# One decoder pass on one core: attention, mLSTM and HGRN products of two heads in turn on the halves of TensorE, GpSimd left out of some stretches, larger first loads

## The chip, the core and the metric

The kernel runs on one core of a Trainium2 chip. It is launched once, reads all inputs from HBM and writes one output of 256 x 1024 numbers. The metric is the device time of an execution in microseconds (us): the median of the runs shown. A profile is one execution taken by the hardware profiler; its time is given beside it.

The engines of the core have short names in the rows: PE is TensorE (matrix products; PEld its weight loads), DVE is VectorE, ACT is ScalarE, POOL is GpSimd, SP issues most DMAs. Each has its own stream of instructions, which it works through in the order of the program; semaphores order them against each other.

## What is computed

Two transformer blocks run one after the other on 256 tokens of width 1024 (T = 256, D = 1024). All is fp32 from outside. The reference, cut to its order of calls:

```python
def first_block(x, mem, ...):
    h = token_mixer(rmsnorm(x, norm_mix_pre), w_in, b_in, ...)       # mLSTM, short conv, MoBA attention, HGRN2; 4 heads of 64 each
    x = x + rmsnorm(h, norm_mix_post)
    h = memory_cross_attention(rmsnorm(x, norm_cross_pre), rmsnorm(mem, mem_norm), wq, wk, wv, wo)   # 4 heads of 128
    x = x + rmsnorm(h, norm_cross_post)
    h = conv_glu_ffn(rmsnorm(x, norm_ffn_pre), w_ffn_in, conv_w, conv_b, w_ffn_out)                  # width 2816
    return x + rmsnorm(h, norm_ffn_post)

def second_block(x, ...):
    h = x + hybrid_mixer(rmsnorm_2(x, norm_mix), w_in, fox_f_bias, ...)   # fox: 8 heads, causal with decay; nsa: 8 heads, two key groups
    h = h + peer_ffn(rmsnorm_2(h, norm_ffn), wq, subkeys, u, v)           # 128 x 128 experts, 8 heads, top 16
    return rmsnorm_2(h, norm_final)
```

In an attention head the scores are q k^T over a head width of 64, a bias is added (MoBA: a relative bias with mask; fox: a decay c_t - c_s and the causal mask; nsa: the causal mask), a softmax over the row follows, and the probabilities multiply the values, again 64 wide. mLSTM forms such a matrix with exponential gates in place of a softmax, and HGRN2 forms one from the decayed products of its gates.

## The kernel before

Activations lie transposed: features on the 128 partitions, eight blocks of them, and the 256 tokens along the free dimension. A dense product of fp32 weights and activations is three products in the format float32r: each operand is split in a high half (a rounded copy) and a low half (the rest), and `mm3` (lines 342 to 347) does high x high (L345), high weight x low activation (L346) and low weight x high activation (L347). `fm_pair` makes two blocks of 128 output features, 48 such products.

Weights stream through `whalf` (L315): a DMA on SP's queue brings 512 KB (tile w), ScalarE copies the high half (wh, recorded at L366 as all of ScalarE's work), and the low half (wl, L324) is w - wh, made by GpSimd for every third half (`wi % 3 == 2`) and by VectorE for the others. Four buffers of each let this run ahead of the products. In the two expert stages at the end `uvnext` (L1040 on) does the same with the expert matrices (uv, uvh, uvl at L1048).

The stages follow each other: start and first norm; `block1_mixer`; `cross`; `ffn`; `block2`; `peer_q`; `peer`. A normalization needs the sum over all features. `norm_sums` (L450) squares four pairs of blocks on ScalarE and adds them on GpSimd (L463); a product with a constant matrix (onesd, L466) sums over partitions, and `rstd` (L432) with three VectorE steps makes the root. At the end of a sub-layer `post_pair` (L489) does this for its output, and `post_norm` (L520) updates x in four pairs (L537, L538; the last pair on GpSimd) and makes the two halves of the next input, xnh on ScalarE and xnl on VectorE (L542). The order of VectorE's work is written out by hand there. `head_norm` does the like for heads.

The order of the instructions on each engine is fixed when the program is built: a planner (`schedule_with_timeline_sim`) simulates the times of all engines and picks what is ready; `issue_after` and `self.behind` force one instruction behind another. Generators (moba, lstm, levels, fox, nsa, memory, cmp) let the source weave steps of attention between dense products.

`attention` (L1626) is used three times: moba (one pair of chunks, 4 heads), fox (two pairs, 8 heads), nsa (two pairs, 8 heads, two branches). A chunk `ch` holds two heads, one in partitions 0 to 63 and one in 64 to 127. A step takes the two heads in the same half `i` of two chunks. Its `scores` (L1642) multiply 64 rows by 128 queries against 128 keys for the first block of queries (S0) and 256 for the second (S1); biases are added by further products into the same PSUM tile (moba L1479; fox decay L811 with 128 rows of LT and RT, most of them zero; causal mask L814); `softmax_rows` (L1620, L1624) and four scalings follow. `values` transposes the probabilities (L1665), copies them (attPT, by ScalarE) and multiplies them with the values into 64 partitions of `po` (L1671, L1672). There are 2 steps for moba, 4 for fox and 8 for nsa. While the scores of a step are worked on by VectorE and ScalarE, the values of the step before and dense products run on TensorE.

HGRN's decay levels (L1423) already take the two heads of a chunk in turn, one in each row half. mLSTM (L1488 on) goes head by head: its gate rows (L1492), its scores (L1500, L1501), then for two heads the numerator and the denominator (L1513, L1514). HGRN's output is three products per head (L1562 to L1564).

At the start (L596 on) x comes in four DMAs of 256 KB and the first weights in two, in turn; each row of such a DMA is 2 KB.

## Time and profile before

| what | value |
|---|---|
| runs, us | 1524.4, 1528.95, 1523.76; median 1524.4 |
| profiled execution, us | 1525.86 |
| its span (first to last instruction), us | 1524.0 |
| TensorE busy | 1477.3 us, 97% |
| VectorE busy | 1078.9 us, 71% |
| ScalarE busy | 777.5 us, 51% |
| GpSimd busy | 323.5 us, 21% |
| mean granted TensorE clock | 0.988 of 2.4 GHz |
| moved by DMA | 246.6 MB, mean 162 GB/s |

Busy shares are means over stages that have different limits, so the table only says where to look. A busy TensorE is one with a product in flight: products are pipelined, and the duration of one (0.28 us for 256 columns in float32r) is longer than the distance between the starts of two. The profile names what ended each wait. On TensorE an fp32 product is recorded as two instructions, a float32r one as one.

### The profile page before, as it was taken

What the parts mean: (1) busy time and instruction counts of PE and PEld (TensorE: products, weight loads), DVE (VectorE), ACT (ScalarE), POOL (GpSimd) and SP (SyncE); (2) the same over time, 40 slices, a digit from 0 to 9 for tenths busy, and PEclk for the clock granted to TensorE, in tenths of its full rate; (3) what the DMA queues carried; (4) which work ended last, traced back from release to release, by engine and by line L of the source; (5) the groups of instructions that cost most, each with busy time, mean ns of one, the idle gap of its engine ahead of it and who ended that gap; (6) DMA issues with size and microseconds to landing.
All of it is one profiled execution on the core that took longest, in us unless ns stands there. A gap on an engine that the chain in (4) does not pass through costs nothing.

```text
span 1524.0 us, 26760 instructions
## 1 busy us (share of the span) xinstructions
PE 1477.3 (97%) x10594; PEld 1364.8 (90%) x10594; DVE 1078.9 (71%) x1930; ACT 777.5 (51%) x1311; POOL 323.5 (21%) x193
## 2 busy tenths in 40 slices
PE   7999989999999999998999999999999999999997
PEld 6888978999998888898999999999999888888886
DVE  6768677766777455557997988878887555555555
ACT  5536556444555555446454545544445555555554
POOL 3733343323224241116352220000000000000001
PEclk9999989999999999999999999999999999999999
DMA  7442432455653353346255455545546555555553
GB/s 239 133 166 92 155 114 77 151 190 178 193 170 125 111 161 100 101 150 230 78 163 186 159 163 177 168 163 167 166 165 205 197 193 193 194 193 193 194 194 124
DMA packets 68679, 246.63 MB, mean 162 GB/s; under 512 B 7589, under 2 KB 8617, under 8 KB 68297
## 3 DMA queue, kind: packets, MB, share of 16 engines
q1 hardware_dynamic: 67976, 243.08, 48.4%
q8 instruction: 83, 1.36, 0.4%
q10 hardware_dynamic: 576, 1.84, 0.3%
q14 instruction: 44, 0.35, 0.1%
HBM read 242.79 MB, written 2.10 MB: 161 GB/s over the span
## 4 chain that ended last, share of the span: by engine, by line
PE 72%; DVE 10%; ACT 2%; DMA 1%; issue 1%; POOL 1%; SPq 0%; DVEq 0%; ACTq 0%; POOLq 0%
PE acc L345 19%; PE acc L346 19%; PE acc L347 19%; PE att L346 3%; PE att L347 3%; PE att L345 3%; PE att L1194 2%; DVE wl L324 1%; DMA uv<-in_U_dram 1%; PE att L1642 1%; DVE xnl L542 1%; PE acc L1671 1%; DVE uvl L1048 1%; DVE tmp L988 1%; POOL uvl L1048 1%
## 5 line engine op out<-in xcount | busy, mean ns | idle before, releaser
L1048 DVE TENSOR_TENSOR uvl<-uv,uvh 128x1024 fp32r<-128x1024 f32 x234 | 289.5, 1238 | 155.1 <-ACT uvh L366 154.9
L366 ACT ACTIVATE uvh<-uv 128x1024 fp32r<-128x1024 f32 x256 | 270.1, 1056 | 232.4 <-PE acc L346 125.2
L366 ACT ACTIVATE wh<-w 128x1024 fp32r<-128x1024 f32 x187 | 195.7, 1056 | 231.1 <-PE acc L346 101.7
L345 PE MATMUL acc<-hh,uvh 128*128 128x256 f32 x1024 | 293.9, 287 | 0.0
L347 PE MATMUL acc<-hh,uvl 128*128 128x256 f32 x1024 | 289.9, 283 | 1.5 <-DVE uvl L1048 1.0
L346 PE MATMUL acc<-hl,uvh 128*128 128x256 f32 x1024 | 289.8, 283 | 0.0
L324 POOL TENSOR_TENSOR wl<-w,wh 128x1024 fp32r<-128x1024 f32 x63 | 158.2, 2511 | 353.0 <-ACT wh L366 320.8
L324 DVE TENSOR_TENSOR wl<-w,wh 128x1024 fp32r<-128x1024 f32 x124 | 165.0, 1337 | 79.2 <-ACT wh L366 76.2
L346 PE MATMUL acc<-uvl,ch 128*128 128x512 f32 x512 | 199.2, 389 | 0.0
L347 PE MATMUL acc<-uvh,cl 128*128 128x512 f32 x512 | 199.2, 389 | 0.0
L347 PEld LDWEIGHTS acc<-hh,uvl 128*128 128x128 f32 x1024 | 195.9, 191 | 2.6 <-POOL uvl L1048 1.3
L346 PEld LDWEIGHTS acc<-hl,uvh 128*128 128x128 f32 x1024 | 196.1, 191 | 0.0
L345 PEld LDWEIGHTS acc<-hh,uvh 128*128 128x128 f32 x1024 | 196.0, 191 | 0.0
L345 PE MATMUL acc<-xnh,wh 128*128 128x256 f32 x544 | 162.4, 299 | 8.4 <-ACT xnh L366 8.4
L346 PE MATMUL acc<-xnl,wh 128*128 128x256 f32 x544 | 161.0, 296 | 6.0 <-DVE xnl L340 3.7
L347 PE MATMUL acc<-xnh,wl 128*128 128x256 f32 x544 | 158.3, 291 | 0.0
L345 PE MATMUL acc<-uvh,ch 128*128 128x512 f32 x512 | 138.5, 389 | 0.0
L1273 POOL TENSOR_TENSOR fin<-fin,gn 128x512 f32<-128x512 f32 x4 | 5.2, 1288 | 588.2 <-ACT sq L366 588.1
L345 PEld LDWEIGHTS acc<-xnh,wh 128*128 128x128 f32 x544 | 107.9, 199 | 11.8 <-ACT xnh L366 8.9
L346 PEld LDWEIGHTS acc<-xnl,wh 128*128 128x128 f32 x544 | 108.0, 198 | 10.4 <-DVE xnl L340 5.4
L346 PE MATMUL att<-xnl,wh 128*128 128x256 f32 x368 | 106.4, 289 | 8.6 <-DVE xnl L542 8.6
L346 PEld LDWEIGHTS acc<-uvl,ch 128*128 128x128 f32 x512 | 96.1, 188 | 20.0
(440 smaller groups left out, 3161.5 us busy)
## 6 DMA issues: line engine op xcount, KB each, us to landing
w<-in_W_dram SPq DMA_DIRECT2D x191, 512.0 KB, 4.0
uv<-in_U_dram SPq DMA_DIRECT2D x128, 512.0 KB, 3.6
uv<-in_V_dram SPq DMA_DIRECT2D x128, 512.0 KB, 3.5
x<-in_xT_dram SPq DMA_DIRECT2D x4, 256.0 KB, 6.3
mem<-in_memT_dram SPq DMA_DIRECT2D x1, 1024.0 KB, 6.5
sk<-in_W_dram SPq DMA_DIRECT2D x1, 1024.0 KB, 7.2
xd<-xt SPq DMA_DIRECT2D x2, 512.0 KB, 5.2
fin<-xd ACTq DMA_DIRECT2D x2, 512.0 KB, 7.2
```

Source lines behind the costliest of these rows:

```text
L324: (self.nc.gpsimd if pool else self.nc.vector).tensor_tensor(out=lo, in0=w, in1=hi.bitcast(F32), op=ALU.subtract)
L345: mm(ps, wsl(w[0]), xsl(x[0]), start=first, stop=False, **k)
L346: mm(ps, wsl(w[0]), xsl(x[1]), start=False, stop=False, **k)
L347: mm(ps, wsl(w[1]), xsl(x[0]), start=False, stop=last, **k)
L366: return self.nc.scalar.activation(out, in_, f, **k)
L542: nc.vector.scalar_tensor_tensor(n.halves[1][:, k], x[:, k], gain[:, k:k + 1], n.halves[0][:, k].bitcast(F32), op0=ALU.mult, op1=ALU.subtract)
L988: nc.vector.match_replace(tmp[:, :n], vals[:, 0:8], src, -3.0e38)
L1048: i = (nc.gpsimd if lo_pool else nc.vector).tensor_tensor(out=lo, in0=w, in1=hi.bitcast(F32), op=ALU.subtract)
L1194: mm(ps[:, j], m1[:, j], m2[:, s * NT + j], start=s == 0, stop=s == 1)
L1273: nc.gpsimd.tensor_tensor(out=half[b][n], in0=half[b][n], in1=gn[:, n * 512:(n + 1) * 512], op=ALU.mult)
L1642: mm(S[:, c], q[r, ch, blk * 128:(blk + 1) * 128], k[r, br if nsa else ch, :128 * (blk + 1)], start=c == 0, stop=False, skip_group_check=True)
L1671: mm(po[r, c], v[:, 0, vc:vc + 64], PT[:, 0:256], start=not nsa, stop=False, skip_group_check=True)
```

## The change

1. `attention`: a step now takes the two heads of one chunk. Scores, fox decay and values of the two heads are issued in turn, on the two row halves (scores, decay) or column halves (values) of the array; each head has its own PSUM tile for scores. The second to fourth products of a group are put behind the first. For the decay, LT and RT hold their rows twice, once in each half. The maxima and sums of the softmax are taken per head and block of queries.
2. mLSTM: the scores of two heads, and then numerator and denominator, alternate in the same way. HGRN's output products alternate between heads.
3. A flag `calm`: while it is set, no low half of a weight is made by GpSimd. It is set at the start, from the end of the mixer to the queries of cross attention, from its output product until the FFN's fourth step, from the FFN's step 19 or output product 8 until fox attention begins, and from the output product of block 2 until the first query pair of PEER; in the other PEER pairs every second half (before: every third) goes to GpSimd.
4. The sums of squares (L463, L500), the product of two gains and the last pair in `post_norm` move from GpSimd to VectorE.
5. Start: x comes in two DMAs of 512 KB and the first weights in one (rows of 4 KB); eight products of constants are issued on TensorE before anything has landed.

```diff
@@ constants
-        er[h, h] = 1.0
-        el[32 + h, h] = -1.0
+        er[h, h] = er[64 + h, h] = 1.0
+        el[32 + h, h] = el[96 + h, h] = -1.0
@@ whalf
-        pool = self.wi % 3 == 2
+        pool = not self.calm and self.wi % self.every == self.every - 1
@@ norm_sums (post_pair the same)
-                nc.gpsimd.tensor_tensor(out=s, in0=s, in1=sq, op=ALU.add)
+                nc.vector.tensor_add(s, s, sq)
@@ post_norm
-                    eng = nc.gpsimd if p == 3 else nc.vector
-                    eng.tensor_tensor(out=hp, in0=hp, in1=bc, op=ALU.mult)
-                    eng.tensor_tensor(out=xp, in0=xp, in1=hp, op=ALU.add)
+                    nc.vector.tensor_mul(hp, hp, bc)
+                    nc.vector.tensor_add(xp, xp, hp)
@@ build (ones and onesd are now set here, and loads follow)
+                idle = self.att((128, T))
+                for _ in range(8):
+                    nc.tensor.matmul(idle, self.onesd, self.ones, start=True, stop=True)
-                for j in range(4):
-                    if j % 2 == 0:
-                        part = slice(j * 256, j * 256 + 512)
-                        nc.sync.dma_start(w[:, part], self.a["W"][0][:, part])
...
-                    nc.sync.dma_start(x[:, 2 * j:2 * j + 2], self.a["xT"][:, j * 512:(j + 1) * 512])
...
+                for j in range(2):
+                    nc.sync.dma_start(x[:, 4 * j:4 * j + 4], self.a["xT"][:, j * 1024:(j + 1) * 1024])
+                    if j == 0:
+                        nc.sync.dma_start(w, self.a["W"][0][:, :1024])
...
@@ block2
-                act(LT[0:8], z[0:8, 2][:, None, :].to_broadcast([8, 8, T]), AF.Copy)
-                act(RT[32:40], z[32:40, 2][:, None, :].to_broadcast([8, 8, T]), AF.Copy)
+                for i in (0, 64):
+                    act(LT[i:i + 8], z[0:8, 2][:, None, :].to_broadcast([8, 8, T]), AF.Copy)
+                    act(RT[i + 32:i + 40], z[32:40, 2][:, None, :].to_broadcast([8, 8, T]), AF.Copy)
...
-                    mm(S, LT[:, h, blk * 128:(blk + 1) * 128], RT[:, h, :128 * (blk + 1)], **flags)
+                    r = slice(64 * (h % 2), 64 * (h % 2) + 64)
+                    mm(S, LT[r, h, blk * 128:(blk + 1) * 128], RT[r, h, :128 * (blk + 1)], **flags)
@@ peer_q, after norm_sums
+                self.calm, self.every = False, 2
@@ mlstm
+                    ps = [self.att((128, 384)) for _ in range(2)]
+                    for blk in range(2):
+                        for i, (h, r) in enumerate(heads):
+                            mm(ps[i][:, 256 * blk:256 + 128 * blk], mk[r, c, blk * 128:(blk + 1) * 128], mq[r, c, blk * 128:],
+                               start=True, stop=True)
...
+                    for o_ in (pn, pd):
+                        for blk in range(2):
+                            for h, r in heads:
+                                l = vt[:, blk, 256 + h * 64:320 + h * 64] if o_ is pn else self.ones[:, :64]
+                                mm(o_[r, 128 * blk:], l, W[:, h, 256 * blk:256 + 128 * blk], start=blk == 0, stop=blk == 1)
@@ attention
+        def scores(ch, br):
+            S = [self.att((128, 384)) for _ in range(2)]
+            order = [(blk, i) for blk in (1, 0) for i in (1, 0)]
+            first = None
+            for blk, i in order:
+                with self.behind(first):
+                    m = mm(S[i][:, part[blk]], q[rows[i], ch, blk * 128:(blk + 1) * 128],
+                           k[rows[i], br if nsa else ch, :128 * (blk + 1)], start=blk == 1, stop=False, skip_group_check=True)
+                first = first or m
+            for n, add in enumerate(bias):
+                for blk, i in order:
+                    add(S[i][:, part[blk]], 2 * ch + i, blk, dict(start=False, stop=n == len(bias) - 1, skip_group_check=True))
...
+            for i in range(2):
+                for blk in (1, 0):
+                    nc.vector.tensor_reduce(st[:, 0, i, blk:blk + 1], S[i][:, part[blk]], AX.X, ALU.max, negate=True)
+                    self.act(P[:, i, part[blk]], S[i][:, part[blk]], AF.Exp, bias=st[:, 0, i, blk:blk + 1],
+                             accum_out=st[:, 1, i, blk:blk + 1])
...
+            for blk in range(2):
+                for i in (1, 0):
+                    vc = (br * 128 + 64 * i) if nsa else (2 * ch + i) * 64
+                    with self.behind(first):
+                        m = mm(po[rows[i], ch % 2, 128 * blk:], v[:, blk, vc:vc + 64], PT[i][:, 256 * blk:256 + 128 * blk],
+                               start=not nsa and blk == 0, stop=blk == 1, skip_group_check=True)
+                    first = first or m
```

## Rows read from the trace of the kernel before

**Rows 1.** The page: TensorE's busy time, and its granted clock in 40 slices (tenths).
```profile
PE 1477.3 (97%) x10594; PEld 1364.8 (90%) x10594; DVE 1078.9 (71%) x1930; ACT 777.5 (51%) x1311; POOL 323.5 (21%) x193
...
PEclk9999989999999999999999999999999999999999
```

**Rows 2.** TensorE's waits at seams A, C, D, E: total us, times, longest.
```profile
PE att L346 <- DVE xnl L542: 4.7, 3, 2.3
...
PE att L346 <- DVE xnl L542: 3.9, 4, 2.6
...
PE acc L346 <- DVE xnl L542: 2.2, 3, 1.2
...
PE att L474 <- DVE rstd L448: 3.2, 1, 3.2
PE acc L345 <- ACT xnh L366: 1.6, 1, 1.6
```

**Rows 3.** Stretches: length, PE, PEld, DVE, ACT, POOL busy; clock; DMA share; GB/s.
```profile
0.00:6.50 6.50, 0.00 (x0) 0.00 (x0) 1.57 (x6) 1.67 (x3) 1.90 (x14) 1.00 0.63 142
6.50:16.50 10.00, 6.51 (x19) 4.57 (x19) 8.71 (x10) 8.15 (x15) 6.61 (x4) 1.00 1.01 398
...
198.00:214.00 16.00, 11.11 (x60) 9.89 (x59) 12.42 (x11) 8.29 (x14) 9.08 (x5) 0.79 0.31 99
...
252.00:265.00 13.00, 10.43 (x78) 10.23 (x77) 12.79 (x17) 6.98 (x13) 7.49 (x5) 0.87 0.12 42
...
300.00:325.00 25.00, 25.00 (x212) 25.00 (x211) 14.03 (x21) 10.46 (x14) 7.22 (x3) 1.00 0.57 184
...
600.00:625.00 25.00, 25.00 (x183) 21.76 (x182) 13.31 (x27) 12.79 (x29) 4.79 (x2) 1.00 0.27 87
...
704.00:726.00 22.00, 18.51 (x127) 18.19 (x128) 14.92 (x26) 13.25 (x22) 14.91 (x8) 0.84 0.77 261
```

**Rows 4.** In order of time (start, us), then groups of instructions (count, busy, mean ns).
```profile
9.73 4.54 POOL L463 TENSOR_TENSOR sq<-sq 128x512 f32<-128x512 f32 x3 [5.29 <-ACT sq L366]
10.21 7.26 DVE L340 SCALAR_TENSOR_TENSOR xnl<-x,vec,xnh 128x256 fp32r<-128x256 f32 x5
196.39 0.87 DVE L542 SCALAR_TENSOR_TENSOR xnl<-x,vec,xnh 128x256 fp32r<-128x256 f32 x2
203.58 4.77 DVE L542 SCALAR_TENSOR_TENSOR xnl<-x,vec,xnh 128x256 fp32r<-128x256 f32 x4
...
L324 POOL TENSOR_TENSOR wl<-w,wh 128x1024 fp32r<-128x1024 f32 x63 | 158.2, 2511 | 353.0 <-ACT wh L366 320.8
L324 DVE TENSOR_TENSOR wl<-w,wh 128x1024 fp32r<-128x1024 f32 x124 | 165.0, 1337 | 79.2 <-ACT wh L366 76.2
...
L366 ACT ACTIVATE LT<-fz 8x2048 f32<-8x2048 f32 x1 | 1.9, 1896 | 0.0
```

**Rows 5.** The chain that ended last, block 2's attention: start us, us, what.
```profile
536.34 1.51 PE att L811 x8
...
541.72 0.58 PE acc L1671 x2
542.29 0.22 PE acc L1672 x2
...
582.76 1.50 PE att L1642 x8
```

**Rows 6.** TensorE in order of time: HGRN's levels, then its output product.
```profile
66.54 1.16 PE L1423 MATMUL att<-hqk 64*128 64x128 f32 x16
67.63 0.39 PE L345 MATMUL acc<-xnh,wh 128*128 128x256 f32 x1
...
115.60 0.27 PE L1564 MATMUL att<-hA,vt 128*64 128x128 f32 x1
115.66 0.27 PE L1563 MATMUL att<-hAo,vt 128*64 128x128 f32 x1
```

**Rows 7.** TensorE in order of time: the first norm's sum at the start.
```profile
18.76 1.91 PE L466 MATMUL att<-sq,onesd 128*128 128x256 f32 x4
```

## Prediction of the changed kernel's time

> **What bounds the kernel now.** I read the page first, then a table of stretches, then TensorE's waits, then single stretches in order of time. TensorE (PE) is busy for 97% of the span [rows 1], and its clock line shows few slices under full speed: the kernel is bound by TensorE's instruction stream, with losses at a handful of places. So an edit is worth something only if it makes that stream shorter, or fills a hole in it. From about 770 us to the end (the two expert stages, half of the span) the change touches nothing; everything has to come out of the time before.
>
> The holes lie at the start and at four seams, where one stage's last sum must be normalized before the next can begin: mixer to cross attention (198 to 214 us, seam A), cross to FFN (252 to 285, C), FFN to block 2 (464 to 482, D), block 2 to the PEER queries (684 to 726, E). In each, TensorE waits for VectorE (DVE), mostly for the low halves of the normalized input (xnl) [rows 2], and the mean granted clock falls to 0.79 to 0.87 at A, C and E [rows 3], so what is not idle there runs partly at 1.2 instead of 2.4 GHz. Why VectorE is late can be read in the DVE rows: two xnl steps take 0.87 us (0.43 each) while GpSimd rests, but four take 4.77 and five take 7.26 (1.2 to 1.45 each) where GpSimd works through tensor operations of its own at the same time [rows 4]. Between the seams, in block 1's mixer and in block 2's attention, TensorE has no holes; there its instructions themselves are the cost [rows 5].
>
> **Part 1: two heads side by side on TensorE.** What running side by side is worth can be seen in this trace, for HGRN's decay levels already alternate between the two row halves: 16 instructions of 64 rows and 128 columns start at 66.54 and the next full-array one at 67.63, 1.09 us for all [rows 6]. A scores step of attention has 8 such instructions (each fp32 product is two): four of 128 columns, four of 256, all in one row half, and takes 1.50 us on the chain [rows 5]. With a slot of 0.112 us for 128 columns and 0.216 for 256, serial is 4 x 0.112 + 4 x 0.216 = 1.31, and 0.19 is left for entering and leaving the half-array form. The same slot explains HGRN: 8 pairs x 0.112 = 0.90, and 0.19 left. So a paired step should take 2 x 0.112 + 2 x 0.216 + 0.19 = 0.85: 0.65 saved. There are 14 steps (moba 2, fox 4, nsa 8): 9.1 us. The fox decay (1.51 us per step now, full rows [rows 5]) is cut to half rows and joins the paired group without an entry of its own: 1.51 - 0.66 = 0.85, four times: 3.4. For column halves the evidence is HGRN's output product, whose instructions start 0.06 us apart [rows 6], half of a slot. The values step costs 0.58 + 0.22 per head on the chain [rows 5], 1.60 for two; paired 0.85 by the same sum, 0.75 saved where the heads lie apart. I take 0.7, times 14: 9.8. The mLSTM scores become two paired groups instead of four single ones (4 x 0.85 - 2 x 0.85): 1.7. Its numerator and denominator already change column half between heads, so a part overlaps: between 0 and 1.4 us for each of two groups, taken as 0.5: 1.0. HGRN's output is side by side already: 0. Sum 25.0, of which 5.4 in block 1 and 19.6 in block 2.
>
> Does it come off the end? In block 2 the chain is TensorE's own instructions, and VectorE and ScalarE are busy for half of a stretch such as 600 to 625 [rows 3], so I count nine tenths: 17.6. In block 1 many short dependent VectorE and ScalarE steps lie beside, and a shorter TensorE stream may meet them; bounds 0 and 5.4, taken 3.5. The other edits here: a scores step has four smaller reductions instead of two, one reciprocal less, about +0.1 us of VectorE, hidden by the dense products that run between scores and values; two more ScalarE copies of the decay rows, 1.9 us each [rows 4], hidden while key and value products run ahead of the first decay, worth 3.8 us if that cover went. The pinned order ("behind") makes three products of a group wait behind the first; queued behind them on TensorE is whatever the planner put there, usually dense products that need nothing of them.
>
> The Trainium skill (TensorEngine Tiling (Array Packing), PSUM Bottleneck under Performance Considerations) warns that tiling speeds TensorE but not the emptying of PSUM, which can become the bound. By that rule part 1 in block 2 would give nothing; its price is in the third rival, and the trace speaks mostly against it.
>
> **Part 2: GpSimd quiet at the seams.** All low halves of weights (wl), the sums of squares and the last quarter of the residual update go to VectorE there. A wl costs 2.51 us on GpSimd and 1.34 on VectorE [rows 4]. At seam A GpSimd works 9.08 of 16 us, VectorE 12.42 [rows 3]. Moved, GpSimd's share is about 9.08 x 1.34 / 2.51 = 4.8 us of VectorE; on the last four xnl alone VectorE gets back 4.77 - 1.74 = 3.0 [rows 4]. So its sum rises by 1.8 at most, and what it takes over (sums of squares, later weights) can follow the xnl, for which the products wait. The most that each seam can give back is its wait and its lost clock: A 4.7 + 0.21 x 16 = 8.1; C 3.9 + 0.13 x 13 = 5.6; D 2.2 without its clock; E 1.6 + 3.2 + 0.16 x 22 = 8.3 [rows 2, 3]. I take 7, 4.5, 2 and 2.5, together 16.0 of 24.2. E gets the least: its larger wait (3.2) is for rstd, and there GpSimd still makes low halves of the first expert weights, which the change leaves on it, and after the first query pair it gets every second wl instead of every third. That last edit I cost at nothing: no wait of TensorE is shown between 726 and 770. Elsewhere in the quiet stretches VectorE takes over some 20 wl (a third of about 60). I cost them at nothing too: TensorE's products hide them, for it needs two wl, 2.7 us, only every 48 dense products, 5.7 us (212 in 25 us at 300 to 325 [rows 3]); without that cover they are 27 us. Lower bound of the part: 0, if VectorE is then the late one.
>
> **Part 3: the start.** Eight extra fp32 products run before any load lands. One instruction of that shape takes 0.43 us there (four in 1.91 [rows 7]; 0.216 at full speed), so 16 of them are 6.9 us from about 1.3 us on: TensorE's first useful product moves from 6.9 us to about 8.2. In return the clock can be up when it starts, where now the lower level still holds at 18.8 us. The loads come as 512 KB pieces; the first product now needs 1.17 MB of them instead of 0.63. The rate was 142 GB/s up to 6.5 us and 398 from there to 16.5 [rows 3], so these land between about 5.5 and 10.6 us. After that VectorE paces: five xnl at 0.43 instead of 1.45 give back 5.1 us [rows 4], less one wl (1.34) and three sums (0.67 each, half a wl) that it takes over: 1.8. The most to be had is TensorE's idle time and half of its busy time from 6.5 to 16.5 us, 3.5 + 3.3 = 6.8 [rows 3]; the worst, with the loads at 10.6, some 2 lost. The next stage hangs on rstd, which follows the sums; I take 4.
>
> **Sum.** 17.6 + 3.5 + 16.0 + 4 = 41.1 us. The profiled execution took 1525.9 us (span 1524.0), 1.5 above the median of 1524.4; so 1525.9 - 41.1 = 1484.8 on its own scale, 1483 on the median's.
>
> **Rivals.**
> *The pairs come apart.* The order on each engine is fixed by a planner; where it puts dense products or a wait between the two halves, nothing overlaps. For it: before, the scores of a step stand split in several places. Against: the second to fourth products are tied to the first, which uses the buffer that is taken last. Then 17.6 + 3.5 are lost: 1504.
> *VectorE becomes the bound at the seams.* It had 12.42 of 16 us at A and takes more. Against: what it loses to GpSimd's company is as large as what it takes over. Then 16.0 are lost: 1499.
> *Emptying PSUM is the bound in block 2.* VectorE is busy 13.3 and ScalarE 12.8 of 25 us at 600 to 625 [rows 3], so a step of about 10.5 us has 5.6 of VectorE in it; TensorE would have to fall under that, and it falls by 1.4. Only by latency can it bind. Then 17.6 are lost: 1501.
> *Slower: TensorE stalls in every attention step.* Both heads' probabilities, transposes and copies must now be there before the first product of the values step; before, the first head's product could start while the second's copy ran. If the planner's dense product stands in front of the scores and not between scores and values, each of the 14 steps waits out reduction, exponential, scaling and copy, some 4 us, and 1.7 us of clock as at seam C: 80 us, 1563. It decides the sign from about 3 us per step on. Against it: dense products stood in between in every step shown.
>
> **How the numbers follow.** Forecast 1483: 0.66, with a range of its own from 1472 to 1495. Pairs apart 0.08, VectorE at the seams 0.12, PSUM 0.06, the first two together (1520) 0.04, slower 0.04. A measurement here can tell about 0.5%, 7.6 us, from no change; so faster 0.92, same 0.04, slower 0.04. The range 1470 to 1504 reaches over the forecast with its unknown terms and the three rivals beside it.
>
> **What would show it.** Right: in the chain of the profile after, a scores step takes 0.85 us instead of 1.50, and fox's joined group about 1.5 instead of 3.0; xnl takes 0.43 each in every seam, with GpSimd idle beside it; the clock at A and C stays at 1.0; dense products start 0.12 us apart from about 9 us on. Wrong: scores or values in groups of two with other lines between; waits of TensorE for copies of the probabilities or for wl; a stretch with VectorE busy throughout at a seam; a clock under 1 in block 2.

## The result, and the profile after

The changed kernel takes 1499.2 us (median of four runs, 1496.0 to 1500.0) against 1524.7: ratio 0.9823, 95% interval 0.980 to 0.985. So 25.5 us are gone where 41 were forecast. One run of a later kernel (the last but one, under seam E) took 2354.4 us at a mean granted clock of 0.555, where its other runs had 0.99, and is left out of its median. The profiled execution took 1499.6 us (span 1497.7, 26.3 under before's 1524.0).

Lines of the page after: busy time by engine, then the granted clock in 40 slices.

```profile
PE 1451.0 (97%) x10610; PEld 1348.4 (90%) x10610; DVE 1087.2 (73%) x1992; ACT 781.6 (52%) x1313; POOL 232.9 (16%) x145
...
PEclk9999999999999999999999999999999999999999
```

TensorE is busy 26.3 us less than in [rows 1], exactly what the span lost: its idle time is what it was. Waits of before are gone, and others stand in their place. TensorE's waits after (total us, times, longest):

```profile
PE acc L348 <- ACT uvh L369: 4.0, 1, 4.0
PE att L477 <- DVE rstd L451: 3.8, 1, 3.8
PE acc L348 <- ACT wh L369: 3.1, 2, 2.8
PE att L349 <- DVE xnl L544: 2.9, 3, 2.0
PE att L857 <- ACT attPT L369: 2.7, 2, 1.8
PE att L469 <- DVE sq L466: 2.5, 1, 2.5
```

Against [rows 2], the waits for xnl at the seams fell from 10.8 in total (4.7 + 3.9 + 2.2) to 2.9, and the wait for rstd stayed. New are a wait for the first expert weights (uvh), one for a sum of squares (sq), and several for transposed probabilities (attPT).

Stretches after, in the columns of [rows 3]: seam A; the first part of seam C; the four stretches at half clock behind waits at seam C, in the fox attention, at seam E and at the start of the expert stage; the first 10 us with data.

```profile
191.70:207.70 16.00, 14.84 (x110) 13.76 (x108) 13.88 (x21) 8.65 (x13) 0.00 (x0) 1.00 0.54 171
238.00:251.00 13.00, 10.60 (x87) 10.19 (x87) 12.12 (x23) 6.08 (x13) 0.00 (x0) 1.00 0.22 81
257.80:261.20 3.40, 3.40 (x19) 3.40 (x18) 2.60 (x6) 0.63 (x2) 0.73 (x1) 0.50 0.66 217
534.30:541.10 6.80, 6.09 (x28) 4.67 (x27) 2.64 (x8) 2.89 (x10) 2.54 (x2) 0.50 0.42 142
687.90:694.70 6.80, 4.66 (x21) 4.64 (x22) 5.73 (x9) 3.10 (x7) 4.00 (x3) 0.50 0.65 224
749.30:752.80 3.50, 3.09 (x14) 3.09 (x15) 3.50 (x17) 1.85 (x4) 2.50 (x2) 0.51 0.47 150
...
6.50:16.50 10.00, 7.23 (x50) 6.04 (x49) 9.80 (x18) 8.27 (x16) 2.19 (x1) 1.00 1.03 408
```

At seam A GpSimd rests (0.00 busy) and the clock is 1.00 where it was 0.79. The four half-clock stretches show what a wait can cost besides itself: each begins in one of TensorE's waits or within 1.5 us behind it and lasts 3.4 to 6.8 us, of which half is lost. Not every wait has one: behind the wait of 2.0 us for xnl at 246.7 the clock stays at 1.00 until 257.8.

The paired steps in the chain after (start, us, what): a joined step of scores and decay, then a selected-attention step's scores and values.

```profile
514.99 0.85 PE att L1661 x8
515.85 0.66 PE att L824 x8
...
552.05 0.85 PE att L1661 x4
553.40 0.85 PE att L1661 x4
...
573.85 0.85 PE att L1661 x8
...
578.67 0.80 PE acc L1696 x8
```

The scores of two heads take 0.85 us where they took 1.50, and scores with decay 1.51 where they took 3.0 [rows 5]. The two rows x4 are the first step of the selected attention: there the planner put dense products between the two heads, and each head takes 0.85 us by itself. In fox's first step the short products came apart too. The other twelve of the 14 steps are whole.

To see where the gain went I marked the same TensorE instruction in each trace and compared the time between marks. In brackets: the mark's time before. Each entry is the change of a stage's length in us, from one profiled execution:

| stage, up to its mark | forecast | after | Part 1 alone | Part 2 alone | without Part 3 |
|---|---|---|---|---|---|
| start and mixer, last output product (197.8) | -7.5 | -6.3 | -0.1 | -3.8 | -5.6 |
| seam A, first cross scores (219.1) | -7 | -7.6 | -0.8 | -7.5 | -7.5 |
| cross, last output product (243.6) | 0 | +0.4 | -1.1 | +0.5 | +0.4 |
| seam C and FFN, last input product (433.5) | -4.5 | -0.1 | 0.0 | -1.9 | 0.0 |
| seam D, last gate product (484.8) | -2 | -3.7 | 0.0 | -3.7 | -3.7 |
| fox attention, last dense product that makes the values (563.3) | -7.3 | -1.2 | -1.2 | -0.6 | -1.8 |
| selected attention, last product (674.4) | -10.3 | -11.7 | -11.6 | 0.0 | -11.6 |
| seam E, last use of rstd by TensorE (720.7) | -2.5 | +0.4 | -0.1 | +0.4 | +0.2 |
| queries, last product (759.7) | 0 | -1.8 | -0.7 | -1.6 | -1.7 |
| expert stage, first index transpose (800.7) | 0 | +6.2 | +4.5 | +6.1 | +6.2 |
| rest | 0 | -1.0 | -0.7 | -0.8 | -0.7 |
| span | -41.1 | -26.3 | -11.9 | -12.8 | -25.9 |

The forecast's 17.6 for block 2 is split by its own terms. The last of fox's four values steps lies behind the mark in both kernels (571.6 before, 554.3 after), so fox has nine tenths of the sum of 4 x (0.65 + 0.85) and 3 x 0.7, and the selected attention nine tenths of the sum of 8 x (0.65 + 0.7) and 0.7.

Executions of one kernel differ by some 10 us, so a stage in one profile is not its mean: seven kernels here have after's code in the first row's stage, and it is 0.7 to 6.3 us shorter than before in them, 4.1 on average. Rows that repeat in every kernel with the same code there (seam A, seam D, selected attention) are firm. The medians below come from different chips, on which the kernel before takes 1521.3 to 1526.0 us, so kernels are compared by their ratios to it. The intervals of all runs that start from the kernel after, 0.3 to 0.4% to either side, overlap that of after: none of these edits shows in the time alone, and what it does is read from the stages.

### The profile page after: what moved, and what is told of

Read it like the earlier page. It is cut to its first block, busy times and chain, and to the rows that moved or that the text cites. A ratio compares the mean times of both kernels' runs of the same rounds, so it can differ in the third digit from the quotient of the medians.

```text
span 1497.7 us, 26770 instructions
## 1 busy us (share of the span) xinstructions
PE 1451.0 (97%) x10610; PEld 1348.4 (90%) x10610; DVE 1087.2 (73%) x1992; ACT 781.6 (52%) x1313; POOL 232.9 (16%) x145
## 4 chain that ended last, share of the span: by engine, by line
PE 74%; DVE 10%; ACT 2%; issue 1%; DMA 0%; ACTq 0%; DVEq 0%
PE acc L348 20%; PE acc L349 20%; PE acc L350 19%; PE att L349 3%; PE att L348 3%; PE att L350 3%; PE att L1210 2%; DVE wl L327 1%; DVE uvl L1064 1%; PE att L1661 1%; DVE tmp L1003 1%; PE acc L1696 1%; ACT wh L369 1%; DVE ti L1005 1%; DVE ti L1006 1%
## 5 line engine op out<-in xcount | busy, mean ns | idle before, releaser
L327 DVE TENSOR_TENSOR wl<-w,wh 128x1024 fp32r<-128x1024 f32 x144 | 183.5, 1281 | 86.5 <-ACT wh L369 85.2
L327 POOL TENSOR_TENSOR wl<-w,wh 128x1024 fp32r<-128x1024 f32 x43 | 107.3, 2497 | 375.9 <-ACT wh L369 330.6
L348 PE MATMUL acc<-xnh,wh 128*128 128x256 f32 x544 | 158.8, 293 | 4.6 <-ACT wh L369 3.1
L349 PE MATMUL acc<-xnl,wh 128*128 128x256 f32 x544 | 156.0, 287 | 0.1
L350 PEld LDWEIGHTS acc<-uvh,cl 128*128 128x128 f32 x512 | 96.1, 188 | 19.9
L348 PEld LDWEIGHTS acc<-uvh,ch 128*128 128x128 f32 x512 | 96.1, 188 | 19.9
```

The costliest lines, as they stand in the source:

```text
L327: (self.nc.gpsimd if pool else self.nc.vector).tensor_tensor(out=lo, in0=w, in1=hi.bitcast(F32), op=ALU.subtract)
L348: mm(ps, wsl(w[0]), xsl(x[0]), start=first, stop=False, **k)
L349: mm(ps, wsl(w[0]), xsl(x[1]), start=False, stop=False, **k)
L350: mm(ps, wsl(w[1]), xsl(x[0]), start=False, stop=last, **k)
```

## The experiments

### Each part by itself

Part 1 alone is the kernel before with the new attention, mLSTM and HGRN code and the doubled decay tables; nothing else.

> The kernel before with Part 1 alone (pairs of heads in attention, mLSTM and HGRN; GpSimd and the start as before). By the forecast's terms 17.6 us in block 2 and 3.5 in block 1 go: 21.1, about 1503.5. By the trace of after, where block 2 is only 13.4 us shorter although each scores step takes 0.85 us and each values step 0.80 as forecast: TensorE's new waits there (0.93 + 1.77 + 0.71 + 0.65 for attPT behind ScalarE's table loads, and 7 us at half clock) belong to Part 1 itself, so they are here too: 16 to 18 us, 1507 to 1509. Rival: the waits come from VectorE's and GpSimd's new shares (Part 2) and are not here: 20 us or more.

Measured: 1514.2 us, ratio 0.9936 (0.9912 to 0.9959), some 10 us. Less than either theory, but the stages say which one holds: the selected attention gives its 11.6 us and fox only 1.2, as in after. Another 4.5 us were lost at the start of the expert stage, where this edit changes nothing. So the fox losses belong to Part 1.

Part 2 alone has the `calm` flags, the sums, the residual updates and `every = 2`, with attention and start as before.

> The kernel before with Part 2 alone (GpSimd quiet at the seams, every second wl in the expert queries). By the forecast's terms 16.0 us: 1508.5. By the milestones of after: seam A -7.5, C -2, FFN +2, D -3, E +0.7, queries -2, start of the expert stage +5.4: some 6 to 7 us, 1518. Rival: the losses at E and at the start of the expert stage come from the shifted timing of block 2 (Part 1), then 11 us or more.

Measured: 1514.9 us, ratio 0.9943 (0.9924 to 0.9962), between the theories. Seams A and D give all that they give in after, E nothing. And 3.8 us come in the first stage: with GpSimd quiet the xnl at the start take 0.43 us each here. The 6.1 us at the start of the expert stage are lost here too, so they don't come from block 2's new timing.

Part 3 alone has the eight products ahead of the loads and the loads of 4 KB rows:

> The kernel before with Part 3 alone (eight products ahead of the loads, loads of 4 KB rows). Forecast's term 4 us: 1520.5. By the trace of after the clock is up at 5.2 us, but rstd ends 0.6 us later than before and TensorE then waits 2.8 us for wh at 37.4 and runs at half clock from 39.4 to 46.2: gain 0 to 1 us, 1523.5 to 1524.5. Here GpSimd is not quiet at the start, so the five xnl cost 1.45 us each and not 0.43: by that 0, or some 2 us lost.

Measured: 1521.3 us, ratio 0.9993 (0.9969 to 1.0016): no difference that can be told. Its profiled execution had lost 8.8 us by the end of the mixer (span 1534.8), so its stages say little. By their medians the three parts alone give 10.3, 9.6 and 3.2 us, 23 together, and after gives 25.5; by the ratios 9.8, 8.7 and 1.1, 20 together, against 27. So the sum is shown to some 7 us only, and the loss at the start of the expert stage stands in each part (4.5, 6.1 and 5.2) and in after once (6.2). The complement is after without Part 3:

> The kernel after without Part 3: no products ahead of the loads, the first loads in pieces of 2 KB rows as before; Parts 1 and 2 as in after. Theory: Part 3 adds nothing to a quiet GpSimd, because Part 2 alone was 7.1 us ahead of before at 88 us of its span and after, with both, 6.8: within 2 us of after, and TensorE's wait for wh at 37.4 us and the half clock from 39.4 to 46.2 are not there. Rival, the forecast's term: Part 3 is worth 4 us of its own, so about 4 us slower than after, 1503.

Measured: 1500.1 us, ratio 0.983 (0.980 to 0.986), against 0.9823 with it. The first 10 us with data, and TensorE's waits in this kernel:

```profile
6.50:16.50 10.00, 9.14 (x33) 7.51 (x34) 8.37 (x16) 7.99 (x16) 0.72 (x1) 1.00 1.01 394
...
PE acc L348 <- ACT xnh L369: 7.0, 2, 6.6
```

Without Part 3 TensorE begins at 6.6 us and has started 33 instructions by 16.5, its products 0.21 us apart; with it 47 (the row's 50 has the last three of the idle products), 0.12 us apart. The clock of 1.00 in the row without Part 3 is no reading: that profile's first record of the clock stands at 15.7 us, and the products go from 0.21 to 0.12 us apart at 16.0. The same holds for the first two rows of [rows 3], where the first record stands at 22.4. Yet after then waits 2.8 us for wh at 37.4, and the lead of 14 instructions is one of 5 at 37 us and a lag of 9 at 40. At the end of the mixer the two stand 0.7 us apart. The wait for wh is not there without Part 3, as the theory said; a stretch at half clock is there in both, from 39.4 to 46.2 with Part 3 and from 43.0 to 49.8 without. Part 3 is worth nothing that shows.

### What makes the pairs overlap

```diff
-            order = [(blk, i) for blk in (1, 0) for i in (1, 0)]
+            order = [(blk, i) for i in (1, 0) for blk in (1, 0)]
```

> The kernel after with one edit: in the scores step the products go head by head (both blocks of one head, then both of the other) and not in turn between the row halves; the same instructions on the same halves. Theory: only neighbours in the queue on different halves run side by side, so a scores step takes 1.3 to 1.5 us again in place of 0.85, and the fox decay steps 1.2 to 1.3 in place of 0.68: 14 x 0.5 to 0.65 and 4 x 0.5 to 0.6, 9 to 11.5 us more than after, about 1509. Rival: TensorE overlaps the halves whatever their order: 0.85 stays, 1499.

Measured: 1500.7 us (two runs), ratio 0.9855 (0.9812 to 0.9898), and in the chain:

```profile
576.44 0.86 PE att L1661 x8
```

The rival holds: 0.86 us though both products of one head stand ahead of both of the other in the instruction stream. In the trace the 256-column products of the two halves start 13 ns apart (7 in after), with a 128-column product of the first half between them in the stream, which starts only 0.5 us later. What before lacked was not the alternation, but the second half's work near by: its steps held one row half each. How near is not tested; where dense products on the full array stand between, as at 552.05 and 553.40 in after, nothing overlaps. The Trainium skill (TensorEngine Tiling (Array Packing), Key Properties) says that tiles operate independently; this run agrees, and shows that it reaches past the next instruction.

### Where fox's gain went

After, ScalarE in order of time in the last fox steps:

```profile
531.23 1.28 ACT L369 ACT_TABLE_LOAD   x1
532.52 0.26 ACT L369 ACTIVATE hid<-hid 128x64 f32<-128x64 f32 x1
532.68 0.61 ACT L369 ACTIVATE yh<-yf 128x512 fp32r<-128x512 f32 x1
533.21 0.47 ACT L369 ACTIVATE attPT<-att 128x384 f32<-128x384 f32 x1
533.69 1.28 ACT L369 ACT_TABLE_LOAD   x1
...
535.45 0.48 ACT L369 ACTIVATE attPT<-att 128x384 f32<-128x384 f32 x1
```

The compressed keys' Gelu (hid) brings two table loads, and one of the two heads' copies stands behind each; TensorE waits for them at 532.0 and 535.3 (1.77 and 0.71 us). Its wait at 530.8 (0.65) is for hid on VectorE and not for a copy.

```diff
-                    act(hid, hid, AF.Gelu)
+                    act(hid, hid, AF.Copy)
```

> The kernel after, with the Gelu of the compressed keys' hidden layer left out (a plain copy in its place, so this function is not computed); what goes in time is two table loads of ScalarE (1.28 us each) in the middle of the fox attention. Theory: block 2 gave 13.4 of 17.6 us because these loads make the copies of the transposed probabilities late there: TensorE's waits at 530.8, 532.0 and 535.3 (0.65, 1.77, 0.71) and the half clock from 534.3 to 541.1 (3.4 lost) go: 4 to 6.5 us less at 565 us, 1493 to 1495. Rival: the paired values step needs both heads' copies and waits anyway: within 1.5 us of after.

Measured: fox becomes 5.6 us shorter than before's, not 1.2: 4.4 us. (In the eight kernels with this code and the Gelu it is 1.2 to 3.2 us shorter.) From 520 to 570 us TensorE waits for:

```profile
PE att L968 <- DVE L L964: 1.1, 1, 1.1
PE att L1688 <- DVE hid L889: 0.6, 1, 0.6
PE att L857 <- ACT attPT L369: 0.6, 1, 0.6
```

The 1.77 and 0.71 are gone, and the half clock behind them. In total the run shows none of it (1500.1 us, ratio 0.9825, 0.9796 to 0.9853), and by that interval a gain of 4.4 us can be neither shown nor excluded: this profile lost 5.6 us against after's in the mixer, with a wait of 2.7 us for a DMA (toep<-dr) among it. So the cause is shown by the stage, not by the time. For the other 1.7 us that fox fell short (7.3 - 1.2 - 4.4) there are waits for copies of 0.9 us (at 502.7 in after) and 0.6, and one of 0.6 for hid, in this run too; their causes are not tested.

### The sums of squares

```diff
-                nc.vector.tensor_add(s, s, sq)
+                nc.gpsimd.tensor_tensor(out=s, in0=s, in1=sq, op=ALU.add)
```

> The kernel after with the sums of squares ahead of a norm (the adds of norm_sums) on GpSimd again, as before; the rest of Part 2 stays. Theory: at seam C TensorE waits 2.5 us for these sums, queued on VectorE behind the xnl (TensorE's sum of squares starts at 256.4), and loses 1.7 us of clock behind it: up to 4 us less at seam C if the sums run beside, about 1495. Rival: a GpSimd that works beside the xnl makes them 1.2 us each again in place of 0.43, at every seam: 5 us or more lost over A, C, D and E, 1504 or above.

Measured: 1500.3 us, ratio 0.9839 (0.9798 to 0.988). TensorE's waits from 190 to 270 us (seams A and C):

```profile
PE att L349 <- DVE xnl L544: 4.6, 4, 2.0
PE att L469 <- POOL sq L466: 3.1, 1, 3.1
```

Neither theory: TensorE's wait for the sum at seam C is 0.5 us longer with GpSimd than with VectorE, and seam A loses 1.8 us, not 5. VectorE's rows in after show what the waits at seam C hang on:

```profile
246.43 1.23 DVE L327 TENSOR_TENSOR wl<-w,wh 128x1024 fp32r<-128x1024 f32 x1 [0.37 <-ACT wh L369]
247.57 0.68 DVE L540 TENSOR_TENSOR x<-x,hg 128x512 f32<-128x512 f32 x1
...
254.48 1.23 DVE L327 TENSOR_TENSOR wl<-w,wh 128x1024 fp32r<-128x1024 f32 x1
255.63 0.69 DVE L466 TENSOR_TENSOR sq<-sq 128x512 f32<-128x512 f32 x1
```

Low halves of weights stand ahead of the work that TensorE waits for: one ahead of the update of x (TensorE then waits 2.0 us for xnl at 246.7), one ahead of the last sum, whose square was done at 254.97. On GpSimd that sum starts 0.15 us behind its square, but takes 1.72 us and not 0.69. So moving the sum alone gains nothing. What these low halves cost is not tested: no kernel here has them behind the update and the sum.

### The start of the expert stage

The loss there follows from the order of queues. After, in order of time: VectorE's low half of a U tile, SyncE's queue, ScalarE.

```profile
737.75 1.22 DVE L1064 TENSOR_TENSOR uvl<-uv,uvh 128x1024 fp32r<-128x1024 f32 x1
...
738.99 0.33 SPq L1060 DMA_DIRECT2D uv<-in_U_dram  x1
739.37 0.90 SPq L1054 DMA_DIRECT2D xd<-xt  x2
...
746.76 1.28 ACT L369 ACT_TABLE_LOAD   x1 [6.07 <-DVE tq L1005]
```

And before:

```profile
764.75 1.21 DVE L1048 TENSOR_TENSOR uvl<-uv,uvh 128x1024 fp32r<-128x1024 f32 x1
...
766.41 2.19 SPq L1038 DMA_DIRECT2D xd<-xt  x2
...
773.20 1.28 ACT L366 ACT_TABLE_LOAD   x1 [1.02 <-DVE tf L1060]
```

The high half was there at 763.8 before and at 732.3 after: uvl follows 0.95 us later before, 5.4 us after, because VectorE is behind with the top-16 work. The next load of U stands behind uvl in SyncE's queue, the store of the residual (xd) behind that, and the first Gelu, which writes memory that xt held, waits for that store; TensorE's next weights (uvh) are behind the Gelu on ScalarE. The row names a VectorE instruction (tq) as what ended ScalarE's wait, but the second store landed at 746.67, 0.09 us ahead of the table load, and at 773.12 before, 0.08 ahead; in every kernel here that stores from SyncE's queue the two are 0.09 us apart or less. Two edits, each at one link:

```diff
-                self.calm, self.every = False, 2
+                self.calm = False
```

> The kernel after, with GpSimd taking every third low half of weights in the expert queries as before, not every second. Theory: the waits for rstd at 686 (3.8 us) and for uvh at 745 (4.0), with 6.8 and 3.5 us at half clock behind them, come from VectorE being slowed by a GpSimd that is busy for twice as long (VectorE's STT steps of hf took 7.4 us for 8 in place of 4.0): 5 to 10 us less than after, 1489 to 1494. Rival: every wl on GpSimd there hurts alike, or the planner's order does it: within 1.5 us of after, 1498 to 1500.

Measured: 1493.3 us; ratio 0.9822 (0.9789 to 0.9855), the same as after's. (5.8 us under after's median, but this chip's runs of the kernel before spread from 1518.5 to 1530.5 us.) In the profile the expert stage loses 1.4 us, not 6.2, with no wait for uvh, and seam E gains 1.1. VectorE's steps from 690 to 746 us, after and then here:

```profile
L1044 DVE SCALAR_TENSOR_TENSOR hf<-x,vec,rstd 128x256 f32<-128x256 f32 x8 | 7.4, 950 | 0.0
L327 DVE TENSOR_TENSOR wl<-w,wh 128x1024 fp32r<-128x1024 f32 x4 | 7.1, 1775 | 1.0 <-ACT wh L369 1.0
```

```profile
L327 DVE TENSOR_TENSOR wl<-w,wh 128x1024 fp32r<-128x1024 f32 x5 | 6.3, 1266 | 0.0
L1044 DVE SCALAR_TENSOR_TENSOR hf<-x,vec,rstd 128x256 f32<-128x256 f32 x6 | 3.3, 561 | 1.4 <-POOL hl L1046 1.4
```

VectorE does one wl more and is done with them sooner, since a wl costs it 1.27 us in place of 1.78 and an hf 0.56 in place of 0.95. But `every` is not all: Parts 1 and 3 alone leave it as before and lost 4.5 and 5.2 us there, and the run with the sums on GpSimd has every second and lost 1.4. In the profiles with every second and the store on SyncE's queue the stage loses 6.1 to 6.5 us in five and 1.4 in one. With Part 3 alone VectorE's order of work from 710 to 782 us is that of before, and the stage still starts with a 3.2 us wait where before has none. So the wait also falls out differently from one execution to the next.

```diff
-                nc.sync.dma_start(self.xd[b], xt[:, b])
+                nc.scalar.dma_start(self.xd[b], xt[:, b])
```

> The kernel after with one edit: the two stores of the transposed residual (xd<-xt) are issued from ScalarE's queue, not SyncE's. Theory: the first Gelu of the expert stage writes memory that xt held, so it waits until xd has landed; SyncE issues xd late (739.4, 2 us behind the copy) because a load of U ahead of it in the queue waits for uvl on VectorE, and ScalarE holds uvh, TensorE's next weights, behind the Gelu. Issued at about 737.3 and landed some 5.5 us later, the Gelu waits only for VectorE's last match (743.8): 3 us of the 4.0 us wait for uvh go, and part of the 3.5 us at half clock: 3 to 5 us less at 800 us, 1494 to 1496. Rival: VectorE's backlog alone sets it: under 1 us.

Measured: 1497.9 us, ratio 0.9814 (0.9785 to 0.9843). The stage loses 3.5 us, not 6.2; the wait for uvh is 1.1, not 4.0, and ScalarE now waits for VectorE:

```profile
ACT L369 <- DVE tmp L1003: 3.2, 1, 3.2
```

So 2.7 of the 3 to 5 us, and VectorE's backlog is next in line. Both edits together:

> The kernel after with the two edits that shortened the start of the expert stage each by itself: every third low half on GpSimd in the expert queries, and xd<-xt issued from ScalarE's queue. Theory: with every third, VectorE clears the queries' top-16 work earlier (last match 741.1 in place of 743.8) and TensorE's wait for uvh was gone in that run; the stores then land earlier still and that wait stays away in every execution: 4 to 7 us less than after, 1492 to 1495, the best of the kernels here. Rival: the wait comes and goes from one execution to the next, as the kernel before and its run with Part 3 show with the same order of instructions there (0 and 3.2 us): then 1496 to 1499.

Measured: 1495.9 us, ratio 0.9817 (0.979 to 0.9843); no wait for uvh, and the stage again loses 1.4. By its interval it can't be told from after, nor from the run with the first edit alone. What repeats is the stage: the two kernels that are after with every third low half in all query pairs lose 1.4 us there, with no wait for uvh.

### Seam E

Of the three newton steps there, two take long after, beside GpSimd's low halves (5.83 us for two from 683.88 on); the first, which reads one operand from PSUM (att), takes 0.47 us beside them:

```profile
684.92 0.47 DVE L449 SCALAR_TENSOR_TENSOR nt<-att,epsc,rstd 128x256 f32<-128x256 f32 x1
685.43 2.08 DVE L450 SCALAR_TENSOR_TENSOR nt<-nt,rstd 128x256 f32<-128x256 f32 x1
687.54 2.44 DVE L451 SCALAR_TENSOR_TENSOR rstd<-nt,rstd 128x256 f32<-128x256 f32 x1
...
683.88 5.83 POOL L327 TENSOR_TENSOR wl<-w,wh 128x1024 fp32r<-128x1024 f32 x2
```

```diff
-                self.calm, self.every = False, 2
+                self.calm = j < 2
```

> The kernel after with GpSimd kept quiet until the third pair of expert queries (after it makes low halves from the first pair on), and from there every third low half, not every second. Theory: the wait for rstd at seam E (3.8 us at 686.3) is made by two of the three newton steps, which take 2.08 and 2.44 us beside a GpSimd wl, and 0.42 quiet; without it the wait is under 1 us and the half clock behind it (687.9 to 694.7, 3.4 lost) goes too: 5 to 7 us less between 674 and 721 us than after. With every third wl the start of the expert stage loses 0 to 5 us as it falls: 1488 to 1493. Rival: VectorE has three more wl there (1.3 us each) and comes to the expert stage later: the wait for uvh (4.0) grows by as much, and the time is within 2 us of after.

Measured: 1494.3 us (median of three), ratio 0.9808 (0.9766 to 0.9849). TensorE's waits, and a row of GpSimd:

```profile
PE acc L348 <- ACT uvh L369: 4.6, 1, 4.6
...
PE acc L350 <- DVE uvl L1064: 2.6, 2, 1.5
...
PE att L477 <- DVE rstd L451: 1.9, 1, 1.9
...
682.89 3.38 POOL L327 TENSOR_TENSOR wl<-w,wh 128x1024 fp32r<-128x1024 f32 x1
```

GpSimd is not quiet at the seam here: the planner runs a low half of a later query pair there, from 682.89 to 686.27, and the newton step beside it still takes 2.11 us; a wl of 1.21 us on VectorE stands between that step and the last. So the edit tests its theory in part only. Theory and rival each hold in part: the wait for rstd halves, and seam E with the queries is 4.4 us shorter than before's, where after had 1.4. Then the expert stage begins with 8.7 us lost in place of 6.2, with the wait for uvh and a new one for uvl. Most of what was won went to the next queue.

The last run adds the xd store on ScalarE's queue and puts the Gelu's step behind the end of fox in the program:

```diff
-                next(cmp)
                 for _ in fox:
                     pass
+                next(cmp)
```

> The kernel of the run with the quiet GpSimd at seam E, with two edits more: xd<-xt issued from ScalarE's queue, and the Gelu of the compressed keys behind the last step of the fox attention in the program, not ahead of it. Theory: the two table loads leave the fox attention (worth 4.4 us there when the Gelu was left out) and the expert stage starts without the 4 us wait: 4 to 8 us less than that run, 1482 to 1487. Rival: the compressed keys come later and the first selected-attention products wait for them; then as much is lost near 563 us as was won at 535: 1489 to 1492.

Measured: 1501.4 us, ratio 0.9857 (0.9821 to 0.9893): 7 us above the run without, on the same chip, though the intervals overlap. The store on ScalarE's queue again makes the loss at the start of the expert stage smaller, 6.0 us in place of 8.7. The planner left the waits in fox nearly as they were (1.34 and 1.11 us at 534.4 and 536.9), while the selected attention waited 2.98 us for the compressed keys' logits (1.1 in after) and was 9.1 us shorter than before's, not 11.6. The rival in its sign, though not as it had it: little was won in fox, because the edit left the table loads where they hurt.

## Why the prediction was right or wrong

Right in sign and within its range of 1470 to 1504. That is in part luck: the likeliest time was 16 us too low, 1499.2 lies outside the forecast's own range of 1472 to 1495, and the wide range holds it because it reaches over the rivals. It is the time of the rival *VectorE becomes the bound at the seams* (1499), but not by that rival's way: seams A and D gave what was forecast, and two other losses of some 6 us each, in fox and at the start of the expert stage, took its place. Step by step:

- **The slot sum of Part 1 was right to 0.05 us:** 0.85 forecast for scores, 0.85 measured; 0.85 for values, 0.80; 1.5 for the joined group, 1.51. The selected attention gave 11.7 us for 10.3: little hid it, and the tenth that was taken off was not needed.
- **Fox was the mis-sized term of Part 1, 1.2 for 7.3.** The step that failed is "VectorE and ScalarE are busy for half of a stretch": an average of one stretch, 600 to 625, taken for all of block 2. In fox, ScalarE's queue holds two table loads between the copies, and the shorter stream met them: 4.4 us by the run without the Gelu. This is the mechanism of the slower rival (TensorE needs both heads' copies), at one place and not in 14 steps.
- **Seams A and D were right or better** (7.6 for 7, 3.7 for 2), and for the reason given: at A GpSimd is silent, xnl takes 0.43 us and the clock holds. The Trainium skill (SBUF — State Buffer, Who interferes with whom) says that a VectorE instruction with two SBUF inputs contends with a GpSimd one that reads SBUF. The trace agrees in the pairs shown: newton 0.42 alone and 2.08 to 2.44 beside GpSimd, with 0.47 for the step that has one input in PSUM, and hf 0.56 and 0.95.
- **Seam C was wrong, 0.1 for 4.5.** xnl became fast as forecast (0.42 to 0.44 us). The step that failed is "what it takes over (sums of squares, later weights) can follow the xnl": low halves stood ahead of the update of x and of the last sum. So 2.4 us of waits for xnl stayed, and the wait for the sum (2.5) with the clock behind it (1.7) came to them: 6.6 us, where waits and clock had cost 5.6 [rows 2, 3]. That the low halves are the cause is read from the rows and not tested.
- **Seam E was wrong for the reason that lowered it:** GpSimd still works there. 2.5 were taken (the least as a share, of 8.3; in us seam D had less), nothing came.
- **The zero for the end of the queries was, with fox, the largest miss, 6 us.** "No wait of TensorE between 726 and 770" was true, but the wait comes just after it, at the head of the next stage, over VectorE, SyncE, a store and ScalarE. A cover has to be followed to its end, also past the last instruction that the edit touches. How much of it is the work of `every` is open: with every third low half the stage lost nothing, 1.4, 4.5 and 5.2 us in four profiles (store on SyncE's queue). Part of this term is chance: before's profile had no such wait, and kernels with the same order of work there did.
- **The start was wrong by its cause:** Part 3's 4 us are none, and the first stage's gain comes from GpSimd's rest (3.8 us with Part 2 alone). Block 1's pairs give between nothing (alone, -0.1) and 1.8 (without Part 3 against Part 2 alone, 5.6 - 3.8), for 3.5 taken; each figure is one profile's, in a stage that scatters by more than 5 us.
- **Rivals:** the pairs came apart in two of 14 steps (the first of fox and the first of the selected attention). VectorE as the bound holds for C, not for A and D. Emptying PSUM is no bound: against that rule, the selected attention gave more than its forecast.

## What to carry to other kernels

Price a shorter instruction stream step by step, but look at the other engines' queues in each stage it runs in, not at their average: a table load or a long copy inside one of them takes the gain back. A stall that is removed shows the next link of the same chain. When one engine takes over another's work, look where each piece is queued: here low halves of 1.2 us came to stand ahead of an update, a sum and a root that TensorE waited for. And a stage of one profiled execution can stray by 5 us: before such a difference is explained, see how that stage falls out in other kernels that share its code.

## What had not been expected of the hardware

- Products in different row halves overlap although another product of the first half stands between them: 0.86 us in head-by-head order, 0.85 in turn.
- The two stores of the residual (512 KB each) landed 4.8 to 7.5 us after their issue from SyncE's queue, right behind a load of U (eleven kernels), and 2.6 to 4.1 us after their issue from ScalarE's (three kernels).
- A wait of TensorE by 1.8 to 4 us can cost about as much again in clock: behind the four shown in after the clock was at half for 3.4 to 6.8 us, behind one of 2.0 us it stayed up.
